# One-core hybrid decoder step: the feed-forward's opening as one piece in a fixed order, and five plain pairs of up tiles instead of four

## The chip, the core and the metric

One core of one Trainium2 chip runs the whole program. The metric is the device time of one execution in microseconds (us). TensorE does the matrix products, VectorE and ScalarE the elementwise work, GpSimd small copies and some adds, and SyncE issues the DMA transfers. In the profile they are PE (PEld for its weight loads), DVE, ACT, POOL and SP.

## What is computed

The reference is one inference step of a 2-layer decoder trunk on 576 tokens (512 of a prompt, 64 of eight running sequences), width 1024. Each layer has a token-mixing part and a feed-forward part. The change touches the feed-forward alone, all in float32:

```python
xn = rms_norm(x, p['g_pre_ffn'])
u = xn @ p['w_up']                        # 1024 -> 5632
ext = concatenate([conv_prev, u], axis=1)
c = sum(ext[:, j:j + L] * p['w_conv'][j] for j in range(3))
a, b = split(c, 2, axis=-1)
ffn = (gelu(a, approximate=True) * b) @ p['w_down']   # 2816 -> 1024
x = x + rms_norm(ffn, p['g_post_ffn'])
```

## The kernel before

Every float32 matrix is split into a high and a low part in a faster matmul type, and a product is three matmuls: high by high, low by high, high by low. ScalarE makes the high part of a weight tile (a copy, L113), VectorE the low part (a subtraction, L114, `split_w`).

The 5632 up columns are 44 tiles of 128, worked in 22 pairs; a pair's even tile is `a` and its odd tile `b`. The first `NPLAIN` = 4 pairs (tiles 0 to 7) are *plain*: eight weight blocks by three matmuls, over the tokens in two halves of 320 and 256 columns, each half in one of three PSUM banks (`main_bank`, three buffers). VectorE brings a half out of PSUM (L1055, an *evacuation*: two instructions for the first half, one for the second), multiplying by the norm factor `R`. The other 18 pairs are *fast* (`fast_pair`): a Strassen-like scheme makes the pair with seven products of half size in 288 columns (L1162 to L1164; 12 matmuls each) in place of eight. It needs combinations of the weights (`weights`: four additions, four splits) and combinations of the activations, made once a layer by `combine(0..3)`: two normalizations (L1117), four quarter operations (L1118 to L1121), four high parts on ScalarE (L1125) and four low parts on VectorE (L1126), from the x tiles, with the y tiles as scratch.

After a tile is complete, `conv_end` copies its last columns into `cso` on GpSimd (L1068, L1069), ScalarE makes the first tap (L1075), and VectorE adds the other two (L1076, L1077, the *convolution sums*). After the odd tile of a pair `h_tile` follows: gelu on ScalarE (L1086), multiplication on VectorE (L1087), and a split (L1097, L1098). The tile's input buffer `u` has four buffers and is begun by `conv_begin` with a GpSimd copy and a memset (L1041, L1042); the output buffer `c` has two. So tile n's evacuation waits until tile n-4 has had its convolution.

Tiles 0 to 2 are done together in `first_tiles`, inside the end of the token-mixing part. Then `up(j)` runs for each pair, with the down product's tiles (`down`) set between by `FF_AFTER`: in the first group of down tiles, two after each of pairs 4 to 7. `copy_cache` issues two 768 KB cache copies after each pair.

A planner orders the instructions of each engine by a simulated timeline, within data dependences and hand-written edges (`behind`). Inside `tc.manual_schedule(engines=ORDERED)` the instructions of VectorE, ScalarE and GpSimd keep the order in which they are written; TensorE and the DMA queue stay with the planner. Before the change only `boundary_half` uses it. `combine(i)` stands after tile i+3 and behind the newest weight low part.

Of the kernel before, what the change touches and what calls it, by code (L numbers as in the profile page):

```python
# [19 lines left out]
P = 128  # L20
# [59 lines left out]
def trunk_kernel(ctx: ExitStack, tc: tile.TileContext, I, O):  # L80
# [929 lines left out]
    def ffn(l, y, xpool, act, first):  # L1010
# [20 lines left out]
        with ExitStack() as fx:  # L1031
# [6 lines left out]
            def conv_begin(ui):  # L1038
# [14 lines left out]
                def plain(b, hf, t0, n):  # L1053
                    r = R[:, t0:t0 + n]
                    place(t0, n, lambda d, c: V.tensor_tensor(d, c(b), c(r), ALU.mult))  # L1055
                    if hf:
                        conv_end(ui)

                def fast(hf, op, last=False):
                    place(hf * SH, SH, op)  # L1060
# [2 lines left out]
                return plain, fast  # L1063

            def conv_end(ui):
                u = us.pop(ui)
                uv = u[:, 0:80].rearrange("p (b t) -> p b t", t=10)
                G.tensor_copy(cso[:, ui, 0:16].rearrange("p (b t) -> p b t", t=2), uv[:, :, 8:10])  # L1068
                G.tensor_copy(cso[:, ui, 16:18], u[:, NU - 2:NU])  # L1069
                c = cp.tile([P, NU - 2], F32, name="c", tag="c", bufs=2)  # L1070

                def wc(i):
                    o = PR_WC + (l * 2 * NJ + ui) * 3 + i
                    return par[:, o:o + 1]
                S.activation(c, u[:, 0:NU - 2], AF.Copy, scale=wc(0))  # L1075
                V.scalar_tensor_tensor(c, u[:, 1:NU - 1], wc(1), c, ALU.mult, ALU.add)  # L1076
                V.scalar_tensor_tensor(c, u[:, 2:NU], wc(2), c, ALU.mult, ALU.add)  # L1077
                cs[ui] = c
                if ui % 2:
                    h_tile(ui // 2)  # L1080

            hh, hl = [None] * NJ, [None] * NJ

            def h_tile(j):
                ca, cb = cs.pop(2 * j), cs.pop(2 * j + 1)
                S.activation(ca, ca, AF.Gelu_apprx_tanh)  # L1086
                V.tensor_tensor(cb, ca, cb, ALU.mult)  # L1087
# [3 lines left out]
                for hf, d0, d1, c0, c1 in ((0, 0, TS, 0, 80), (0, TS, 320, 80, 336), (1, 0, 256, 336, NU - 2)):  # L1091
                    src, dh, dl = cb[:, c0:c1], hh[j][hf][:, d0:d1], hl[j][hf][:, d0:d1]
                    if c0 == 0:
                        src = src.rearrange("p (b t) -> p b t", t=10)[:, :, 0:8]
                        dh = dh.rearrange("p (b t) -> p b t", t=8)
                        dl = dl.rearrange("p (b t) -> p b t", t=8)
                    S.activation(dh, src, AF.Copy)  # L1097
                    V.tensor_tensor(dl, src, dh.bitcast(F32), ALU.subtract)  # L1098

# [9 lines left out]
            HW = WN // 2  # L1109
            xs, sw = [], None  # L1110

            def combine(i):

                with behind(last_lo[0].ins):
                    x1, x2, ua, ta = (y[4 * (i % 2) + m] for m in range(4))
                    for k, d in ((i, x1), (i + HK, x2)):
                        V.scalar_tensor_tensor(d, xt[k], gnorm(l, 2, k), R, ALU.mult, ALU.mult)  # L1117
                    V.tensor_tensor(ua[:, :SH], x1[:, :SH], x1[:, SH:], ALU.subtract)  # L1118
                    V.scalar_tensor_tensor(ua[:, SH:], x2[:, SH:], -1.0, ua[:, :SH], ALU.mult, ALU.subtract)
                    V.tensor_tensor(ta[:, :SH], x2[:, SH:], x1[:, SH:], ALU.subtract)  # L1120
                    V.scalar_tensor_tensor(ta[:, SH:], ua[:, SH:], -1.0, x2[:, :SH], ALU.mult, ALU.subtract)  # L1121
                    hi, lo = (cp.tile([P, 7 * SH], F32R, name=f"{n}{i}", tag=f"{n}{i}") for n in ("sxh", "sxl"))
                    for src, m, n in ((x1[:, :SH], B11, 1), (x2, B21, 2), (ua, U1, 2), (ta, T3, 2)):
                        cols = slice(m * SH, (m + n) * SH)
                        S.activation(hi[:, cols], src, AF.Copy)  # L1125
                        V.tensor_tensor(lo[:, cols], src, hi[:, cols].bitcast(F32), ALU.subtract)  # L1126
                    xs.append((hi, lo))

            def weights(j):

                r0, r1 = (wp.tile([P, WN], F32, name="wraw", tag="wraw", bufs=3) for _ in range(2))
                for i, r in enumerate((r0, r1)):
                    with behind(last_w[0].ins):
                        last_w[0] = SP.dma_start(r, I["w_up"][l, 2 * j + i])
                ws = cp.tile([P, WN], F32, name="ws", tag="ws")
                a, b = slice(0, HW), slice(HW, WN)
                w0 = split_w(r0, WN, sw, 2)
                V.tensor_tensor(ws[:, b], r0[:, a], r1[:, a], ALU.add)
                V.tensor_tensor(r1[:, a], r1[:, a], r1[:, b], ALU.add)
                V.tensor_tensor(ws[:, a], r0[:, a], r1[:, a], ALU.add)  # L1140
                w2 = split_w(ws, WN)
                w1 = split_w(r1, WN, sw, 2)
                V.tensor_tensor(r0[:, b], r0[:, b], ws[:, a], ALU.add)
                w3 = split_w(r0[:, b], HW)
                return w0, w1, w2, w3

            def fast_pair(j):
                with behind(last_lo[0].ins if j == NPLAIN else None):
                    w0, w1, w2, w3 = weights(j)
                e1, e2 = (conv_begin(2 * j + i)[1] for i in range(2))  # L1150
                with behind(last_mm[0].ins if j == NPLAIN else None):
                    products(w0, w1, w2, w3, e1, e2)

            def products(w0, w1, w2, w3, e1, e2):

# [27 lines left out]
                product(ba, w1, 1, T4, True)  # L1183
                e2(0, lambda d, c: S.activation(d, c(ba), AF.Copy, scale=-1.0), True)

            def up(j):
                if j >= NPLAIN:
                    fast_pair(j)
                else:
                    for ui in (2 * j, 2 * j + 1):  # L1190
                        if ui >= NFIRST:
                            col_tile(load_w(I["w_up"][l, ui]), xh, xl, allk, conv_begin(ui)[0])
                            if ui in COMBINE:
                                combine(COMBINE.index(ui))
                copy_cache()
                copy_cache()

# [9 lines left out]
                col_tile(w, hh, hl, list(range(j0, j0 + nj)), evac)  # L1207

            first_tiles(first, act, [conv_begin(i)[0] for i in range(NFIRST)])
            for j in range(NJ + 1):  # L1210
                if j < NJ:
                    up(j)
                    if j == NPLAIN - 1:

                        xpool.release()
                        sw = right_pool(f"sw{l}")
                else:
                    cp.release()
                    sw.release()
# [228 lines left out]
```

## Time and profile before

| what | value |
|---|---|
| time, median of 3 runs (lowest to highest) | 1683.43 us (1682.94 to 1683.83) |
| the profiled execution: its time, its span | 1681.14 us, 1679.4 us |
| mean granted TensorE clock | 0.985 |
| busy: PE, DVE, ACT, POOL | 1606.9, 1248.1, 877.6, 556.9 us |

How to read it: the span runs from the first to the last instruction; the granted clock is the share of full speed that the chip gave to TensorE (1.00 is 2.4 GHz, 0.50 is 1.2 GHz). Matmuls overlap, so the length listed for one is longer than the step to the next; the steps between starts are what a stretch costs. The same holds for VectorE and ScalarE, whose listed lengths overlap by a little under 0.1 us. Layer 0's feed-forward opens at 446 us and layer 1's at 1277 us.

### The profile page before, as it was taken

To read this page: it belongs to the slowest core of one execution; us is meant where nothing else is said; L and a number is where in the kernel's file an instruction comes from. 1 tells how busy PE (TensorE), PEld (TensorE's weight loads), DVE (VectorE), ACT (ScalarE), POOL (GpSimd) and SP (SyncE) were. 2 spreads that over 40 slices of the span, in tenths; PEclk is the share of its full clock that TensorE was granted. 3 is DMA by queue.
4 is the path that set the end of the run, shared out by engine and by line. 5 is a ranking of instruction groups with operands and counts; after the bars stand their busy time and mean duration, and the time that the engine had idled before them with its cause. 6 is when DMAs were issued, how large, how long until landed. Compare 5 with 4: busy or idle time off the path is not lost.

```text
span 1679.4 us, 35933 instructions
## 1 busy us (share of the span) xinstructions
PE 1606.9 (96%) x14256; PEld 1526.1 (91%) x14256; DVE 1248.1 (74%) x2472; ACT 877.6 (52%) x1638; POOL 556.9 (33%) x800
## 2 busy tenths in 40 slices
PE   8999999999979999999989999989999799999997
PEld 7888997789879999999988899968998799999997
DVE  6775765656898888888757757566568978888985
ACT  6754524564556545555456544255735555555541
POOL 4554332302542111221365553332044411212303
PEclk9999999999989999999999999999999899999999
DMA  5221326848424545653522212378474264456432
GB/s 187 71 71 59 103 100 258 298 181 313 142 102 164 212 159 171 220 200 105 174 80 84 78 65 80 120 280 336 159 272 157 82 213 157 171 200 242 149 119 104
DMA packets 74889, 270.36 MB, mean 161 GB/s; under 512 B 10689, under 2 KB 23265, under 8 KB 73185
## 3 DMA queue, kind: packets, MB, share of 16 engines
q1 hardware_dynamic: 74720, 268.07, 45.0%
q8 instruction: 112, 1.84, 0.4%
q14 instruction: 57, 0.46, 0.1%
HBM read 250.11 MB, written 85.02 MB: 200 GB/s over the span
## 4 chain that ended last, share of the span: by engine, by line
PE 76%; DVE 10%; ACT 5%; POOL 3%; issue 3%; DMA 2%; POOLq 0%; SPq 0%; ACTq 0%; DVEq 0%
PE ps_m L132 14%; PE ps_m L134 13%; PE ps_m L133 13%; PE ps_m L1164 4%; PE ps_m L1162 4%; PE ps_m L1163 4%; DVE wlo L114 2%; PE ps_t L1163 2%; PE ps_t L1164 2%; PE ps_t L1162 2%; PE ps_s L493 2%; DMA wraw<-in_w_up 1%; PE ps_o L965 1%; PE ps_o L869 1%; POOL x L352 1%
## 5 line engine op out<-in xcount | busy, mean ns | idle before, releaser
L113 ACT ACTIVATE whi<-wraw 128x1024 fp32r<-128x1024 f32 (+4 forms) x284 | 247.0, 877 | 209.2 <-PE ps_m L133 55.4
L114 DVE TENSOR_TENSOR wlo<-wraw,whi 128x1024 fp32r<-128x1024 f32 (+4 forms) x284 | 285.4, 1010 | 94.6 <-ACT whi L113 88.3
L132 PE MATMUL ps_m<-xha,whi 128*128 128x320 f32 x864 | 272.4, 316 | 5.4 <-ACT whi L113 3.1
L133 PE MATMUL ps_m<-xla,whi 128*128 128x320 f32 x864 | 270.9, 314 | 0.0
L134 PE MATMUL ps_m<-xha,wlo 128*128 128x320 f32 x864 | 268.4, 314 | 0.5 <-DVE wlo L114 0.5
L132 PE MATMUL ps_m<-xm,whi 128*128 128x256 f32 x864 | 248.6, 288 | 18.5 <-DVE u L1055 18.5
L134 PE MATMUL ps_m<-xm,wlo 128*128 128x256 f32 x864 | 247.8, 287 | 0.0
L133 PE MATMUL ps_m<-xm,whi 128*128 128x256 f32 x864 | 246.9, 286 | 0.0
L132 PEld LDWEIGHTS ps_m<-xm,whi 128*128 128x128 f32 x864 | 165.9, 192 | 22.0 <-issue 20.5
L132 PEld LDWEIGHTS ps_m<-xha,whi 128*128 128x128 f32 x864 | 164.1, 190 | 9.5 <-ACT whi L113 4.3
L1162 PE MATMUL ps_m<-sxh,whi 128*128 128x288 f32 x576 | 170.0, 296 | 0.7 <-ACT acc L1168 0.7
L1163 PE MATMUL ps_m<-sxh,wlo 128*128 128x288 f32 x576 | 169.7, 295 | 0.0
L1164 PE MATMUL ps_m<-sxl,whi 128*128 128x288 f32 x576 | 169.7, 295 | 0.0
L133 PEld LDWEIGHTS ps_m<-xm,whi 128*128 128x128 f32 x864 | 166.1, 192 | 1.5 <-issue 1.1
L134 PEld LDWEIGHTS ps_m<-xm,wlo 128*128 128x128 f32 x864 | 166.1, 192 | 1.1 <-issue 0.2
L133 PEld LDWEIGHTS ps_m<-xla,whi 128*128 128x128 f32 x864 | 164.3, 190 | 2.5 <-issue 2.0
L134 PEld LDWEIGHTS ps_m<-xha,wlo 128*128 128x128 f32 x864 | 163.3, 190 | 2.8 <-issue 1.4
L1069 POOL COPY cso<-u 128x2 f32<-128x2 f32 x88 | 74.4, 845 | 268.3 <-DVE u L1180 199.5
L1162 PEld LDWEIGHTS ps_m<-sxh,whi 128*128 128x128 f32 x576 | 108.4, 188 | 1.2 <-ACT acc L1168 1.2
L1163 PEld LDWEIGHTS ps_m<-sxh,wlo 128*128 128x128 f32 x576 | 108.7, 189 | 0.0
L1164 PEld LDWEIGHTS ps_m<-sxl,whi 128*128 128x128 f32 x576 | 108.3, 188 | 0.0
L1041 POOL COPY u<-cso 128x16 f32<-128x16 f32 x88 | 59.8, 682 | 136.7 <-DVE c L1077 86.9
(342 smaller groups left out, 4187.6 us busy)
## 6 DMA issues: line engine op xcount, KB each, us to landing
wraw<-in_w_up SPq DMA_DIRECT2D x88, 512.0 KB, 3.8
kv<-in_ck SPq DMA_DIRECT2D x32, 768.0 KB, 6.6
kv<-in_cv SPq DMA_DIRECT2D x32, 768.0 KB, 7.0
out_ck<-in_ck SPq DMA_DIRECT2D x32, 768.0 KB, 7.7
out_cv<-in_cv SPq DMA_DIRECT2D x32, 768.0 KB, 6.8
wraw<-in_w_s SPq DMA_DIRECT2D x42, 512.0 KB, 3.6
wraw<-in_w_dn SPq DMA_DIRECT2D x48, 256.0 KB, 2.6
x<-xdr SPq DMA_DIRECT2D x24, 288.0 KB, 6.4
```

What stands on the lines that cost most here:

```text
L113: S.activation(hi[:, :n], raw[:, :n], AF.Copy)
L114: last_lo[0] = V.tensor_tensor(lo[:, :n], raw[:, :n], hi[:, :n].bitcast(F32), ALU.subtract)
L132: PE.matmul(out, ah, bh, start=(i == 0), stop=False)
L133: PE.matmul(out, ah, bl, start=False, stop=False)
L134: last_mm[0] = PE.matmul(out, al, bh, start=False, stop=(i == n - 1))
L352: (V if dram_out and k % 4 == 3 else G).tensor_tensor(xk, xk, yk, ALU.add)
L493: mm = PE.matmul(bp[64 * hh:64 * hh + 64, cp * nh * 32:(cp + 1) * nh * 32], xk[:, c0:c0 + 64], moving(c0), start=True, stop=True)
L1041: G.tensor_copy(uv[:, :, 0:2], cso[:, ui, 0:16].rearrange("p (b t) -> p b t", t=2))
L1069: G.tensor_copy(cso[:, ui, 16:18], u[:, NU - 2:NU])
L1162: PE.matmul(b, wh, xh, start=i == 0 and not more, stop=False, skip_group_check=more)
L1163: PE.matmul(b, wl, xh, start=False, stop=False, skip_group_check=more)
L1164: PE.matmul(b, wh, xl, start=False, stop=i == HK - 1, skip_group_check=more)
```

## The change

`FF_AFTER`, `NPLAIN` and `COMBINE` change, and the opening (from the end of `first_tiles` to the weights of the first fast pair) is written out as one function under `manual_schedule`. `conv_end` is cut into `taps` and `conv_sums`, `h_tile` into `h_gelu`, `h_mult` and `h_split` (all three high parts first, then all three low parts), `combine` into `normalize`, `combine` and `lows`, and `weights` yields once half way. Pair 4 becomes plain, so the fast pairs are 5 to 21. The ten cache copies of the first five pairs are issued behind the opening, and the first down tiles follow pair 5 (two), 6 (three) and 7 (three).

```diff
-FF_AFTER = ({4: 2, 5: 2, 6: 2, 7: 2}, {8: 2, 9: 2, 10: 2, 11: 2}, {12: 2, 13: 2, 14: 2, 15: 2},
+FF_AFTER = ({5: 2, 6: 3, 7: 3}, {8: 2, 9: 2, 10: 2, 11: 2}, {12: 2, 13: 2, 14: 2, 15: 2},
             {17: 1, 18: 1, 19: 1, 20: 1, 22: 4})
-NPLAIN = 4
-COMBINE = (3, 4, 5, 6)
+NPLAIN = 5
...
+            def taps(*uis):
+                for ui in uis:
+                    u = us[ui]
+                    uv = u[:, 0:80].rearrange("p (b t) -> p b t", t=10)
+                    G.tensor_copy(cso[:, ui, 0:16].rearrange("p (b t) -> p b t", t=2), uv[:, :, 8:10])
+                    G.tensor_copy(cso[:, ui, 16:18], u[:, NU - 2:NU])
+                    cs[ui] = cp.tile([P, NU - 2], F32, name="c", tag="c", bufs=2)
+                    S.activation(cs[ui], u[:, 0:NU - 2], AF.Copy, scale=tap_weight(ui, 0))
+
+            def conv_sums(*uis):
+                for i in (1, 2):
+                    for ui in uis:
+                        c = cs[ui]
+                        V.scalar_tensor_tensor(c, us[ui][:, i:NU - 2 + i], tap_weight(ui, i), c, ALU.mult, ALU.add)
+                for ui in uis:
+                    del us[ui]
...
+            def normalize(i):
+                x1, x2, ua, ta = (y[4 * (i % 2) + m] for m in range(4))
+                for k, d in ((i, x1), (i + HK, x2)):
+                    V.scalar_tensor_tensor(d, xt[k], gnorm(l, 2, k), R, ALU.mult, ALU.mult)
...
+            def combine(i, parts, tiles):
+                x1, x2, ua, ta = tiles
+                V.tensor_tensor(ua[:, :SH], x1[:, :SH], x1[:, SH:], ALU.subtract)
+                V.tensor_tensor(ta[:, :SH], x2[:, SH:], x1[:, SH:], ALU.subtract)
+                V.scalar_tensor_tensor(ua[:, SH:], x2[:, SH:], -1.0, ua[:, :SH], ALU.mult, ALU.subtract)
+                V.scalar_tensor_tensor(ta[:, SH:], ua[:, SH:], -1.0, x2[:, :SH], ALU.mult, ALU.subtract)
+                for src, m, n in parts:
+                    S.activation(xs[i][0][:, m * SH:(m + n) * SH], src, AF.Copy)
+
+            def lows(i, parts):
+                for src, m, n in parts:
+                    cols = slice(m * SH, (m + n) * SH)
+                    V.tensor_tensor(xs[i][1][:, cols], src, xs[i][0][:, cols].bitcast(F32), ALU.subtract)
...
                 w2 = split_w(ws, WN)
+                yield
                 w1 = split_w(r1, WN, sw, 2)
                 V.tensor_tensor(r0[:, b], r0[:, b], ws[:, a], ALU.add)
                 w3 = split_w(r0[:, b], HW)
-                return w0, w1, w2, w3
+                yield w0, w1, w2, w3
...
+            def opening():
+                ws, bs, evs = {}, {}, {}
+                halves = [(ui, hf) for ui in range(NFIRST, 2 * NPLAIN) for hf in range(2)]
+                def load(*uis):
+                    for ui in uis:
+                        ws[ui] = load_w(I["w_up"][l, ui])
+                def mm():
+                    ui, hf = halves.pop(0)
+                    col_half(ws[ui], xh, xl, allk, hf, lambda *a: bs.__setitem__((ui, hf), a))
+                def ev(*keys):
+                    for key in keys:
+                        if key[1] == 0:
+                            evs[key[0]] = conv_begin(key[0])[0]
+                        evs[key[0]](*bs.pop(key))
+                        if halves:
+                            mm()
+                with tc.manual_schedule(engines=ORDERED):
+                    load(3, 4, 5)
+                    c = [normalize(0)]
+                    taps(0, 1)
+                    for _ in range(3):
+                        mm()
+                    conv_sums(0, 1)
+                    h_gelu(0)
+                    ev((3, 0))
+                    combine(0, *c[0])
+                    lows(0, c[0][0])
+                    h_mult(0)
+                    ev((3, 1))
+                    h_split(0)
+                    ev((4, 0))
+                    load(6)
+                    c.append(normalize(1))
+                    combine(1, *c[1])
+                    taps(2, 3)
+                    ev((4, 1))
+                    conv_sums(2, 3)
+                    h_gelu(1)
+                    ev((5, 0))
+                    lows(1, c[1][0])
+                    load(7)
+                    ev((5, 1), (6, 0))
+                    h_mult(1)
+                    c.append(normalize(2))
+                    combine(2, *c[2])
+                    h_split(1)
+                    load(8)
+                    ev((6, 1))
+                    lows(2, c[2][0])
+                    taps(4, 5)
+                    ev((7, 0))
+                    load(9)
+                    ev((7, 1))
+                    conv_sums(4, 5)
+                    h_gelu(2)
+                    c.append(normalize(3))
+                    combine(3, *c[3])
+                    xpool.release()
+                    sw = right_pool(f"sw{l}")
+                    ev((8, 0))
+                    lows(3, c[3][0])
+                    h_mult(2)
+                    ev((8, 1), (9, 0))
+                    w = weights(NPLAIN)
+                    next(w)
+                    ev((9, 1))
+                    h_split(2)
+                    early[NPLAIN] = next(w)
+                for ui in range(6, 2 * NPLAIN):
+                    conv_end(ui)
+                for _ in range(2 * NPLAIN):
+                    copy_cache()
...
             first_tiles(first, act, [conv_begin(i)[0] for i in range(NFIRST)])
-            for j in range(NJ + 1):
+            opening()
+            for j in range(NPLAIN, NJ + 1):
```

## Rows read from the trace of the kernel before

**Rows 1.** Stretch; busy us (x instructions) of PE, PEld, DVE, ACT, POOL; granted clock; DMA share, GB/s.

```profile
475.00:480.00 5.00, 0.37 (x3) 0.11 (x1) 5.00 (x9) 2.40 (x4) 1.46 (x1) 0.85 0.00 0
...
485.00:490.00 5.00, 5.00 (x28) 5.00 (x29) 5.00 (x12) 3.04 (x7) 3.17 (x2) 0.62 0.01 3
...
1280.00:1320.00 40.00, 31.39 (x220) 31.15 (x220) 40.00 (x76) 20.35 (x34) 17.20 (x18) 0.88 0.33 126
```

**Rows 2.** Timeline of PE: start, length, what, [idle before it <- releaser]; both holes.

```profile
484.95 0.55 PE L132 MATMUL ps_m<-xm,whi 128*128 128x256 f32 x1 [9.58 <-DVE u L1055]
...
1316.08 0.55 PE L132 MATMUL ps_m<-xm,whi 128*128 128x256 f32 x1 [8.61 <-DVE u L1055]
...
1321.13 0.41 PE L134 MATMUL ps_m<-xm,wlo 128*128 128x256 f32 x1
```

**Rows 3.** Timeline of PE, the two shorter gaps of layer 0's opening.

```profile
462.34 0.35 PE L132 MATMUL ps_m<-xm,whi 128*128 128x256 f32 x1 [0.34 <-DVE u L1055]
...
505.43 0.41 PE L132 MATMUL ps_m<-xha,whi 128*128 128x320 f32 x1 [0.56 <-ACT u L1184]
```

**Rows 4.** Timeline of PE: first matmuls of tile 3, of tile 7, of two products.

```profile
445.98 0.39 PE L132 MATMUL ps_m<-xha,whi 128*128 128x320 f32 x1
...
471.69 0.31 PE L132 MATMUL ps_m<-xha,whi 128*128 128x320 f32 x1
...
489.58 0.29 PE L1162 MATMUL ps_m<-sxh,whi 128*128 128x288 f32 x1
...
491.17 0.29 PE L1162 MATMUL ps_s<-sxh,whi 128*128 128x288 f32 x1
```

**Rows 5.** Timeline of DVE where layer 0's opening begins.

```profile
443.67 3.50 DVE L114 TENSOR_TENSOR wlo<-wraw,whi 128x1024 fp32r<-128x1024 f32 x3
...
447.08 0.75 DVE L1055 TENSOR_TENSOR u<-ps_s,rbc 128x256 f32<-128x256 f32 x2
```

**Rows 6.** Timeline of DVE, one of each kind of step (xN: N together).

```profile
448.07 3.00 DVE L1117 SCALAR_TENSOR_TENSOR y<-x,par,rbc 128x576 f32<-128x576 f32 x4
...
478.70 1.21 DVE L114 TENSOR_TENSOR wlo<-wraw,whi 128x1024 fp32r<-128x1024 f32 x1
...
479.84 0.45 DVE L1119 SCALAR_TENSOR_TENSOR y<-y,y 128x288 f32<-128x288 f32 x1
...
481.71 0.75 DVE L1126 TENSOR_TENSOR sxl<-y,sxh 128x576 fp32r<-128x576 f32 x1
...
482.38 0.82 DVE L1077 SCALAR_TENSOR_TENSOR c<-u,par,c 128x592 f32<-128x592 f32 x1
...
484.26 0.88 DVE L1055 TENSOR_TENSOR u<-ps_m,rbc 128x64 f32<-128x64 f32 x3
...
487.36 0.77 DVE L1087 TENSOR_TENSOR c<-c 128x592 f32<-128x592 f32 x1
...
489.78 0.55 DVE L1098 TENSOR_TENSOR xla<-c,xha 128x64 fp32r<-128x64 f32 x2
...
506.35 1.23 DVE L114 TENSOR_TENSOR wlo<-wraw,whi 128x1024 fp32r<-128x1024 f32 x1 [0.16 <-ACT whi L113]
```

**Rows 7.** Timeline of ACT: tap, high parts of activations, high part of weights.

```profile
447.53 1.47 ACT L1075 ACTIVATE c<-u,par 128x592 f32<-128x592 f32 x2 [0.89 <-DVE u L1055]
...
449.65 1.18 ACT L1125 ACTIVATE sxh<-y 128x576 fp32r<-128x576 f32 x2 [0.28 <-DVE y L1117]
...
505.26 1.06 ACT L113 ACTIVATE whi<-wraw 128x1024 fp32r<-128x1024 f32 x1
```

**Rows 8.** Timeline of POOL: the copy that begins tile 6's buffer.

```profile
478.54 3.97 POOL L1041 COPY u<-cso 128x16 f32<-128x16 f32 x1 [6.77 <-DVE c L1077]
```

**Rows 9.** The same view, a stretch in which the DMA engines are full.

```profile
515.00:520.00 5.00, 5.00 (x41) 5.00 (x40) 3.07 (x4) 2.89 (x6) 0.00 (x0) 1.00 1.12 411
```

**Rows 10.** The same view, at the start of layer 1's opening.

```profile
1275.00:1280.00 5.00, 3.68 (x18) 3.48 (x17) 5.00 (x8) 2.78 (x5) 2.60 (x4) 0.72 0.50 151
```

**Rows 11.** Timeline of PE, the gap in that stretch.

```profile
1276.64 0.71 PE L276 MATMUL ps_t<-con,rr 128*128 128x128 f32 x4 [1.32 <-POOL rr L250]
```

More of the change, by code (lines that the diff above doesn't have):

```diff
@@ L1065, in conv_end @@
             def conv_end(ui):
[L1066 to L1074, printed above, removed]
@@ new lines, in conv_end, with tap_weight @@
+                conv_sums(ui)
+                if ui % 2:
+                    j = ui // 2
+                    h_gelu(j)
+                    h_mult(j)
+                    h_split(j)
+            def tap_weight(ui, i):
+                o = PR_WC + (l * 2 * NJ + ui) * 3 + i
+                return par[:, o:o + 1]
+            def taps(*uis):
[6 more added lines that the diff above has]
+                    S.activation(cs[ui], u[:, 0:NU - 2], AF.Copy, scale=tap_weight(ui, 0))
@@ new lines, in conv_sums, with h_gelu, h_mult @@
+            def conv_sums(*uis):
[5 more added lines that the diff above has]
+                    del us[ui]
+            hh, hl = [None] * NJ, [None] * NJ
+            def h_gelu(j):
+                S.activation(cs[2 * j], cs[2 * j], AF.Gelu_apprx_tanh)
+            def h_mult(j):
+                V.tensor_tensor(cs[2 * j + 1], cs[2 * j], cs[2 * j + 1], ALU.mult)
@@ L1089, in h_tile, with h_split @@
+            def h_split(j):
+                cb = cs.pop(2 * j + 1)
+                del cs[2 * j]
                 i = j % NH
                 _, hh[j], hl[j] = two_parts(fp, i) if i < NEX else two_parts(xp, i - NEX)
[L1091 to L1098, printed above, removed]
+                for part in range(2):
+                    for hf, d0, d1, c0, c1 in ((0, 0, TS, 0, 80), (0, TS, 320, 80, 336), (1, 0, 256, 336, NU - 2)):
+                        src, dh, dl = cb[:, c0:c1], hh[j][hf][:, d0:d1], hl[j][hf][:, d0:d1]
+                        if c0 == 0:
+                            src = src.rearrange("p (b t) -> p b t", t=10)[:, :, 0:8]
+                            dh = dh.rearrange("p (b t) -> p b t", t=8)
+                            dl = dl.rearrange("p (b t) -> p b t", t=8)
+                        if part == 0:
+                            S.activation(dh, src, AF.Copy)
+                        else:
+                            V.tensor_tensor(dl, src, dh.bitcast(F32), ALU.subtract)
@@ L1110, in ffn @@
             xs, sw = [], None
[L1112 to L1127, printed above, removed]
@@ new lines, in normalize @@
+            def normalize(i):
+                x1, x2, ua, ta = (y[4 * (i % 2) + m] for m in range(4))
+                for k, d in ((i, x1), (i + HK, x2)):
+                    V.scalar_tensor_tensor(d, xt[k], gnorm(l, 2, k), R, ALU.mult, ALU.mult)
+                xs.append([cp.tile([P, 7 * SH], F32R, name=f"{n}{i}", tag=f"{n}{i}") for n in ("sxh", "sxl")])
+                return ((x1[:, :SH], B11, 1), (x2, B21, 2), (ua, U1, 2), (ta, T3, 2)), (x1, x2, ua, ta)
+            def combine(i, parts, tiles):
[6 more added lines that the diff above has]
+                    S.activation(xs[i][0][:, m * SH:(m + n) * SH], src, AF.Copy)
@@ L1144, in weights @@
                 w3 = split_w(r0[:, b], HW)
-                return w0, w1, w2, w3
+                yield w0, w1, w2, w3
             def fast_pair(j):
-                with behind(last_lo[0].ins if j == NPLAIN else None):
-                    w0, w1, w2, w3 = weights(j)
-                e1, e2 = (conv_begin(2 * j + i)[1] for i in range(2))
+                w = early.pop(j, None)
+                if w is None:
+                    *_, w = weights(j)
                 with behind(last_mm[0].ins if j == NPLAIN else None):
-                    products(w0, w1, w2, w3, e1, e2)
+                    products(*w, *(conv_begin(2 * j + i)[1] for i in range(2)))
             def products(w0, w1, w2, w3, e1, e2):
@@ L1184, in products @@
                 e2(0, lambda d, c: S.activation(d, c(ba), AF.Copy, scale=-1.0), True)
-            def up(j):
[L1187 to L1194, printed above, removed]
+            early = {}
@@ L1195, in up @@
+            def up(j):
+                fast_pair(j)
                 copy_cache()
```

16 lines of the change are left out of this document (2 added, 14 removed).

## The prediction, made before the changed kernel was run

> **What bounds the kernel now.** I read the busy shares of the page first: TensorE is busy 96% of the span, so only its gaps and its clock can be won, and the slices of the span show its weak places. Two of them lie in the feed-forward's openings, one per layer. Then the windows: in both openings VectorE is busy without a break while TensorE stands still [rows 1]. The timeline of TensorE gives the hole: it stops in tile 7 for 9.58 us in layer 0 and 8.61 us in layer 1, each time released by the evacuation (L1055) of an earlier half, and when it starts again the granted clock is low: a mean of 0.62 over 485 to 490 us, part of it at 1.2 GHz (0.50) and part at 2.4 (1.00) [rows 1, 2]. Two shorter gaps stand beside it in layer 0, of 0.34 and 0.56 us; layer 1 has one like the second [rows 3].
>
> The clock costs as well. In 485 to 490 us, 0.38 x 5 = 1.9 us were lost. In layer 1 the 24 matmuls from 1316.08 to 1321.13 take 5.05 / 23 x 24 = 5.3 us; at full clock 12 matmuls of 288 columns take 1.59 us [rows 4], so 24 of 256 columns take 2.8, and 2.4 were lost. Together the openings lose 9.58 + 0.34 + 0.56 + 1.9 = 12.4 us in layer 0 and 8.61 + 0.56 + 2.4 = 11.6 in layer 1: **24.0 us** is all that can be won here.
>
> Why is the evacuation late? VectorE has work ahead of it that nobody waits for yet (combinations, weight sums), and tile 6's buffer began late: its GpSimd copy took 3.97 us [rows 8]. But VectorE is never idle there. An order cannot shrink its work; it can only put first what TensorE needs.
>
> **The change, part by part.** *Plain for fast.* A plain tile takes (471.69 - 445.98 - 0.34) / 4 = 6.34 us of TensorE [rows 3, 4], a pair 12.7; seven products of 1.59 take 11.1. The change adds 1.6 us of TensorE work per layer. *The plain tiles as cover.* TensorE now has seven plain tiles behind tile 2, not five: work from 445.98 to 490.4 before it must have a combination.
>
> *VectorE's work up to the first product.* It must be done in the written order up to the first weight low part of pair 5. Steps are taken from start to start, which is the listed length less about 0.08 us [rows 6]: normalization 0.73, quarter operation 0.37, low part 0.67 for 576 columns and 0.37 for 288 (as a quarter), convolution sum 0.74, weight low part 1.14, multiplication 0.69, evacuation of a tile 0.80 (0.46 and 0.34), low parts of a split 0.47 + 0.34. From 447.08, where it takes up the first tiles' second halves [rows 5], the list is:
> three second halves 1.0; four combinations of 2 x 0.73 + 4 x 0.37 + 0.37 + 3 x 0.67 = 5.3, so 21.3; twelve convolution sums 8.9; three multiplications 2.1; two splits 1.6; low parts of tiles 6 to 9, 4.6; evacuations of seven tiles but for the last half 5.3; the low part itself 1.1. The sum is **45.9 us**.
>
> *Waits that the order itself makes.* ScalarE keeps its order too: a high part of 576 columns is 0.59, a tap 0.69, a weight's high part 0.96, and a hand-over between the engines adds some 0.1 [rows 6, 7]. Where VectorE's next step needs a result that stands behind others in ScalarE's queue, it waits, and all behind it waits. I walked the list for such places. Before the sums of tile 2: two high parts, the tap and hand-overs (2.1) against one quarter operation and one half evacuation (0.7), 1.4. Before the split of pair 1: two high parts and the first piece against one quarter operation, 1.2. Before tile 8's low part 0.6, and twice 0.15 inside splits. That is 3.5, so the low part ends at 447.08 + 45.9 + 3.5 = 496.5, and TensorE, which started 0.3 us after the release it waited for (evacuations from 484.26, matmul at 484.95) [rows 2, 6], begins the products at 496.8. Its gaps until then are 496.8 - 490.4 = **6.4 us**, in pieces of at most 2.2, since evacuations now come between the combinations.
>
> *The rest of the opening.* After it VectorE has three sums (0.60 each, an estimate from the 576-column row), the second weight's low part, the last evacuation, the split of pair 2, two more low parts and a sum: 6.4, with waits of 1.2 and 0.7 for high parts. Then tiles 6 and 7 must be convolved (3.0) before pair 5's buffers are free, and two evacuations (0.8) before the seventh product: 496.5 + 12.1 + 0.3 = 508.9. TensorE can run six products (9.5) by 506.3, so **2.8 us** more gap (0.2 left out). From there two, three and three down tiles cover the backlog of tiles 8 and 9.
>
> *GpSimd's copies* cost nothing if each begins while VectorE does something that lets it pass; the dearest is 3.97 [rows 8]. In the new order an evacuation follows soon after each convolution, and a waiting VectorE frees it. *The ten cache copies* (7.9 MB) are 19 us at 411 GB/s [rows 9]; behind the last weight load, at some 481, they end at 500, and the down tiles' weights are needed at about 509. I take nothing; without that cover the down tiles come up to 10 us late. *The weight loads* of tiles 6 to 9 and of pair 5 go, as before, into the buffer that the low part three tiles earlier frees, by the walk 10 us and more before they are used: nothing. *The low parts of tiles 3 to 5* lie, as now, in VectorE's gap from 443.67 [rows 5]: nothing.
>
> **Sum.** Per layer 6.4 + 2.8 + 1.6 = 10.8, twice 21.6, against 24.0: **-2.4 us**. On the profiled execution's 1681.14 us that is 1678.7; the median of the runs lies 2.3 higher, at 1683.43, so 1681.0.
>
> Where it can lie: with no waits on ScalarE at all the products begin at 493.3 (gap 2.9), and the seventh product waits 0.7, so 5.6 less per layer. With hand-overs of 0.3 in place of 0.1, some ten on the path, 2 more.
>
> **The rivals.** *A. The walk holds* (0.40): 1681.0, own range 1677 to 1686. *B. ScalarE is never late* (0.25): the walk's waits are filled or shorter. In full 2 x 5.6 more, so 1670; by half 1675. For it speaks that VectorE worked through layer 1's 40 us without a wait [rows 1]; against it, that this was an order made to avoid waits.
>
> *C. The block starts late* (0.13): if tiles 3 to 5 are split only after the first tiles' evacuations, VectorE loses 443.67 to 447.08, 3.4 us, at a point from which it is the bound, and tile 3 starts 3.4 later. Twice 3.4: +6.8 - 2.4 = 4.4 slower, 1687.8. It decides if the first weight low part of the block begins after 447.1. Against it: the halves of the evacuation need `R`, which comes later than the weights.
>
> *D. The clock falls in the small gaps* (0.12). Layer 1's opening fell to 0.72 with no gap above 1.32 us [rows 10, 11]; the walk has 3 us of gaps in the 6 from 494.9. At 1.9 to 2.4 a layer the result is +1.4 to +2.4: 1685 to 1686. The Trainium skill (TensorE: Matmul & The Clock Gate, A second HAM failure mode: psum-queue depth-cycling) describes a kernel whose frequent short idles between groups of matmuls made the clock swing; by that rule both layers pay; if only holes like those of [rows 2] bring the clock down, neither does.
>
> *E. A GpSimd copy holds a tile* (0.10). A copy of 3.97 in place of 0.2 on the path, once a layer, is +7.5 - 2.4: 1688.5. The row shows it outlasting several VectorE instructions [rows 6, 8]. The Trainium skill (SBUF — State Buffer, Who interferes with whom) has a VectorE instruction with two SBUF inputs block a GpSimd read for its whole length; by one instruction it would be 1.1 at most and the sum would move by 2. Against E: VectorE itself waits for that copy, and then gives way.
>
> **The numbers.** A gives faster, same and slower 0.13, 0.24, 0.03; B is faster; C 0.01 same and 0.12 slower; D 0.08 and 0.04; E 0.03 and 0.07. Together 0.38, 0.36, 0.26, where 0.2% (3.4 us) is about what a measurement of this kernel tells from no change. The range 1671 to 1689 leaves out the end of B and mixtures of C with D.
>
> **What would show it.** In the trace after: no gap of TensorE above 2.5 us in either opening; the first product near 497 us and the first of layer 1 some 830 later (the two holes end 831 apart [rows 2]); VectorE waiting for ScalarE about five us in each; the clock at 1.00 from 455 to 515. It is wrong if VectorE waits elsewhere than I listed, if the first half of tile 8 waits over 3 us, or if the down tiles wait for their weights.

## The result, and the profile after

| | before | after |
|---|---|---|
| median of 4 runs each (lowest to highest) | 1683.18 us (1681.22 to 1683.83) | 1695.26 us (1692.94 to 1697.10) |
| ratio, 95% interval | | 1.0065 (1.0048 to 1.0083) |
| span of the profiled execution | 1679.4 us | 1695.3 us |

The change costs 12 us, outside the range that was given. Both layers pay alike. From the first matmul of the opening (`con,rr`) to the first evacuation of the last fast pair, the timelines give 332.7 and 333.4 us before and 340.5 and 341.1 after. That is 7.7 us a layer, 15.5 of the 15.9 between the two spans.

TensorE's timeline of the changed kernel, all gaps in layer 0's opening and the largest one of layer 1's:

```profile
480.96 0.38 PE L131 MATMUL ps_m<-xha,whi 128*128 128x320 f32 x1 [1.68 <-DVE u L1054]
...
491.77 0.36 PE L131 MATMUL ps_m<-xm,whi 128*128 128x256 f32 x1 [0.66 <-DVE u L1054]
...
496.66 0.40 PE L1188 MATMUL ps_m<-sxh,wlo 128*128 128x288 f32 x1 [1.20 <-DVE wlo L113]
...
501.05 0.40 PE L1187 MATMUL ps_m<-sxh,whi 128*128 128x288 f32 x1 [1.21 <-ACT whi L112]
...
502.31 0.40 PE L1188 MATMUL ps_m<-sxh,wlo 128*128 128x288 f32 x1 [0.86 <-DVE wlo L113]
...
505.01 0.40 PE L1188 MATMUL ps_t<-sxh,wlo 128*128 128x288 f32 x1 [0.84 <-DVE wlo L113]
...
515.37 0.63 PE L131 MATMUL ps_m<-xha,whi 128*128 128x320 f32 x1 [3.85 <-ACT whi L112]
...
1354.62 0.64 PE L131 MATMUL ps_m<-xha,whi 128*128 128x320 f32 x1 [3.47 <-ACT whi L112]
```

The first six are the fixed order. The holes of 9.58 and 8.61 us [rows 2] are gone. In their place stand pieces of at most 1.68, and the first product waits for its weight's low part until 496.66. The prediction had said 496.8. VectorE's timeline shows the waits for ScalarE that the prediction had listed as 1.4, 1.2, 0.6 and 1.2, and one more at the end:

```profile
465.12 3.08 DVE L1088 SCALAR_TENSOR_TENSOR c<-u,par,c 128x592 f32<-128x592 f32 x4 [1.18 <-ACT c L1082]
...
477.69 0.73 DVE L1116 TENSOR_TENSOR xla<-c,xha 128x64 fp32r<-128x64 f32 x2 [0.98 <-ACT xha L1114]
...
479.25 1.23 DVE L113 TENSOR_TENSOR wlo<-wraw,whi 128x1024 fp32r<-128x1024 f32 x1 [0.49 <-ACT whi L112]
...
501.03 1.23 DVE L113 TENSOR_TENSOR wlo<-ws,whi 128x1024 fp32r<-128x1024 f32 x1 [1.12 <-ACT whi L112]
...
515.35 0.69 DVE L113 TENSOR_TENSOR wlo<-wraw,whi 128x512 fp32r<-128x512 f32 x1 [3.84 <-ACT whi L112]
```

That last one, and TensorE's gap of 3.85 us beside it, belong to the first down tile. Both name ScalarE's high part (L112) as the releaser, but ScalarE was itself waiting. Its timeline names the transfer:

```profile
514.69 0.63 ACT L112 ACTIVATE whi<-wraw 128x512 fp32r<-128x512 f32 x1 [4.60 <-DMA wraw<-in_w_dn]
```

The timeline of the DMA queue (SP; start, length from the first issue to the end of the last with the waits between, xN: N transfers) says why that load is late:

```profile
472.20 8.63 SPq L1158 DMA_DIRECT2D wraw<-in_w_up  x2
480.88 13.88 SPq L1028 DMA_DIRECT2D out_ck<-in_ck  x12
496.35 8.97 SPq L119 DMA_DIRECT2D wraw<-in_w_dn  x2
```

Twelve cache copies are issued in one go: the opening's ten and the two that follow pair 5, 9.4 MB. Of the 13.88 us, SyncE waits 6.3 for earlier copies to land. Its waits from 480.5 to 495 us (total, times, longest), then the last copy with its time to landing:

```profile
SPq L1028 <- DMA out_ck<-in_ck: 6.3, 4, 2.2
...
494.25 0.51 SPq L1028 DMA_DIRECT2D out_ck<-in_ck  x1
DMA to landing us min/median/max: 19.5/19.5/19.5
```

Taken one by one, the first eight copies go out one after the other, some 0.6 us each (one took 1.04). The ninth goes out at 486.87, when the first has landed (6.0 us after 480.88), and the tenth to twelfth follow the second to fourth. The first down load goes out at 496.35, in good time, but seven copies (5.5 MB) are still on their way, and the last of them lands at 494.25 + 19.5 = 513.8. ScalarE gets the load at 514.69, 18.3 us after its issue. The page, the chain that ended last by line and then two rows of the issues (their last number is the median time to landing):

```profile
PE ps_m L131 13%; PE ps_m L133 13%; PE ps_m L132 13%; PE ps_m L1187 3%; PE ps_m L1188 3%; PE ps_m L1189 3%; DVE wlo L113 2%; DMA wraw<-in_w_dn 2%; PE ps_s L492 2%; PE ps_t L1188 2%; PE ps_t L1189 2%; PE ps_t L1187 2%; DMA wraw<-in_w_up 2%; PE ps_o L964 1%; DVE c L1088 1%
...
out_ck<-in_ck SPq DMA_DIRECT2D x32, 768.0 KB, 11.7
...
wraw<-in_w_dn SPq DMA_DIRECT2D x48, 256.0 KB, 2.6
```

The loads of down weights now stand on the chain with 2% of the span: two loads of some 18 us are 36 us, and that is 2% of 1695. The median of such a load is still 2.6 us, so the row of the issues doesn't show them. The windows of the changed kernel (columns as in [rows 1]) show what the DMA engines moved meanwhile, and a second price:

```profile
445.00:450.00 5.00, 4.78 (x23) 4.78 (x24) 5.00 (x9) 3.12 (x4) 0.85 (x6) 0.66 0.73 237
...
480.00:520.00 40.00, 30.35 (x198) 28.81 (x199) 34.49 (x62) 17.97 (x32) 7.00 (x21) 0.93 0.93 309
...
500.00:505.00 5.00, 2.26 (x13) 1.81 (x13) 3.97 (x9) 3.79 (x8) 0.44 (x2) 1.00 1.08 298
...
510.00:515.00 5.00, 1.52 (x12) 1.29 (x10) 1.51 (x3) 0.40 (x2) 0.31 (x1) 0.91 0.82 277
515.00:520.00 5.00, 4.63 (x18) 4.63 (x19) 4.65 (x7) 3.84 (x8) 1.47 (x3) 0.50 0.81 303
520.00:525.00 5.00, 5.00 (x37) 5.00 (x36) 3.04 (x8) 2.12 (x6) 0.63 (x2) 0.90 0.58 213
```

Over 40 us the DMA engines were nearly full (share 0.93) and moved 309 GB/s in all, not 411. After the wait TensorE starts at a granted clock of 0.50, which is 1.2 GHz. The loss is 0.50 x 4.63 + 0.10 x 5.00 = 2.8 us. So one layer pays 3.85 + 2.8 = 6.7 us; layer 1, with a gap of 3.47 and windows of 0.50 and 0.94 behind it, pays 3.47 + 2.5 + 0.3 = 6.3. Together that is 13.0 of the 15.5 us between the two profiled executions; the other 2.5 are not accounted for.

### The profile page after: what moved, and what is told of

It is laid out like the page before. It is cut to its first block, busy times and chain, and to the rows that moved or that the text cites. A ratio compares the mean times of both kernels' runs of the same rounds, so it can differ in the third digit from the quotient of the medians.

```text
span 1695.3 us, 35939 instructions
## 1 busy us (share of the span) xinstructions
PE 1618.5 (95%) x14280; PEld 1534.0 (90%) x14280; DVE 1243.2 (73%) x2464; ACT 871.3 (51%) x1624; POOL 533.2 (31%) x800
## 4 chain that ended last, share of the span: by engine, by line
PE 74%; DVE 11%; ACT 6%; DMA 5%; POOL 3%; issue 2%; SPq 0%; POOLq 0%; DVEq 0%; ACTq 0%
PE ps_m L131 13%; PE ps_m L133 13%; PE ps_m L132 13%; PE ps_m L1187 3%; PE ps_m L1188 3%; PE ps_m L1189 3%; DVE wlo L113 2%; DMA wraw<-in_w_dn 2%; PE ps_s L492 2%; PE ps_t L1188 2%; PE ps_t L1189 2%; PE ps_t L1187 2%; DMA wraw<-in_w_up 2%; PE ps_o L964 1%; DVE c L1088 1%
## 5 line engine op out<-in xcount | busy, mean ns | idle before, releaser
L112 ACT ACTIVATE whi<-wraw 128x1024 fp32r<-128x1024 f32 (+4 forms) x282 | 245.2, 878 | 190.3 <-PE ps_m L132 52.5
L131 PE MATMUL ps_m<-xha,whi 128*128 128x320 f32 x896 | 285.1, 319 | 15.3 <-ACT whi L112 10.4
L132 PE MATMUL ps_m<-xla,whi 128*128 128x320 f32 x896 | 283.1, 316 | 0.0
L133 PE MATMUL ps_m<-xha,wlo 128*128 128x320 f32 x896 | 280.5, 316 | 0.6 <-DVE wlo L113 0.5
L131 PE MATMUL ps_m<-xm,whi 128*128 128x256 f32 x896 | 256.9, 287 | 1.3 <-DVE u L1054 1.3
L132 PE MATMUL ps_m<-xm,whi 128*128 128x256 f32 x896 | 255.4, 285 | 0.0
L131 PEld LDWEIGHTS ps_m<-xm,whi 128*128 128x128 f32 x896 | 171.4, 191 | 4.2 <-issue 1.8
L132 PEld LDWEIGHTS ps_m<-xm,whi 128*128 128x128 f32 x896 | 171.7, 192 | 1.6 <-issue 1.1
L1188 PE MATMUL ps_m<-sxh,wlo 128*128 128x288 f32 x544 | 161.0, 296 | 4.1 <-DVE wlo L113 4.1
L1187 PE MATMUL ps_m<-sxh,whi 128*128 128x288 f32 x544 | 161.3, 297 | 3.7 <-ACT whi L112 2.4
L1189 PE MATMUL ps_m<-sxl,whi 128*128 128x288 f32 x544 | 160.5, 296 | 0.0
L1088 DVE SCALAR_TENSOR_TENSOR c<-u,par,c 128x592 f32<-128x592 f32 x176 | 144.3, 829 | 5.4 <-ACT c L1082 4.6
L1080 POOL COPY cso<-u 128x2 f32<-128x2 f32 x88 | 48.7, 553 | 259.5 <-DVE u L1205 169.9
```

What stands on the lines that cost most here:

```text
L112: S.activation(hi[:, :n], raw[:, :n], AF.Copy)
L131: PE.matmul(out, ah, bh, start=(i == 0), stop=False)
L132: PE.matmul(out, ah, bl, start=False, stop=False)
L133: last_mm[0] = PE.matmul(out, al, bh, start=False, stop=(i == n - 1))
L1088: V.scalar_tensor_tensor(c, us[ui][:, i:NU - 2 + i], tap_weight(ui, i), c, ALU.mult, ALU.add)
L1187: PE.matmul(b, wh, xh, start=i == 0 and not more, stop=False, skip_group_check=more)
```

## The experiments

The first question was whether the twelve copies are the whole loss, or whether the fixed order or the fifth plain pair also costs. Each ratio is against the kernel before, measured beside it on the same chip, where its median was 1684.5 to 1685.6 us; so the ratios say more than the times. Edits are against the changed kernel unless another is named.

**The copies between the loads.** Two stand behind `load(3, 4, 5)` and two behind each of `load(6)` to `load(9)`; none stand behind the opening.

```diff
                     load(3, 4, 5)
+                    copy_cache()
+                    copy_cache()
...
                     load(6)
+                    copy_cache()
+                    copy_cache()
...
                 for ui in range(6, 2 * NPLAIN):
                     conv_end(ui)
-                for _ in range(2 * NPLAIN):
-                    copy_cache()
```

> The changed kernel, but its ten cache copies go two by two between the weight loads of the opening and not in one burst behind it. Theory 1 (the burst holds back the down tiles' weights and pair 6's weights; each layer's opening ends some 8 us later for it, slow clock included): 1677 to 1683 us, no wait of ScalarE for a down tile's weights above 1 us in the openings, and TensorE's gaps near the 9 us per layer of the walk. Theory 2 (VectorE's fixed order and the extra plain pair cost the time, the late weights only fill time that would be lost anyway): 1692 to 1697 us. In between, 1685 to 1690, if both.

Measured: 1683.35 us, just above the range of theory 1, ratio 0.9998 (0.9987 to 1.0009). The queue now issues two copies after each load, and the same gaps of the fixed order are there. Queue, then TensorE:

```profile
482.14 1.15 SPq L1028 DMA_DIRECT2D out_ck<-in_ck  x2
486.07 20.52 SPq L119 DMA_DIRECT2D wraw<-in_w_dn  x2
```

```profile
482.21 0.38 PE L131 MATMUL ps_m<-xha,whi 128*128 128x320 f32 x1 [1.68 <-DVE u L1054]
...
497.92 0.40 PE L1188 MATMUL ps_m<-sxh,wlo 128*128 128x288 f32 x1 [1.20 <-DVE wlo L113]
```

The waits for down weights are gone, and with them the whole loss: 1.0065 against 0.9998 is 11.3 us. In layer 0 the first evacuation of pair 8 comes 118.6 us after the opening's first matmul, against 126.3 in the changed kernel: 7.7 us, where 6.7 were worked out above. What is left of the change measures as nothing.

**The copies later.** The opening issues none; a third copy follows each pair from 8 on. It was run twice.

```diff
                 copy_cache()
                 copy_cache()
+                if j > 7:
+                    copy_cache()
```

> The changed kernel without copies in the opening: the ten follow later, one more behind each of the pairs from 8 on. Theory 1: 1676 to 1682 us, like the run with copies between the loads or a little under it, as no copy then shares the DMA engines with the opening's weight loads. Theory 2: 1692 to 1697 us. If copies between the loads cost as well, this one is faster than that one by more than 3 us.

> The run with the copies later once more, beside the next one on the same chip: 1680 to 1684 us, a ratio to before of 0.998 to 1.000.

Measured: 1682.95 us, ratio 0.9988 (0.9974 to 1.0003), and 1683.82, 0.9995 (0.9984 to 1.0006); the first time lies above its range. With no copy in the way at all it is no better than with two behind each load: what counts is that they do not stand together.

**The burst in the kernel before.** The same twelve copies at one point, behind the weights of pair 5; the order and the plain pairs stay as they were.

```diff
-                copy_cache()
-                copy_cache()
+                for _ in range(0 if j < 5 else 12 if j == 5 else 2):
+                    copy_cache()
```

> The kernel before with only its cache copies moved: those of pairs 0 to 5, twelve in all, go in one burst behind pair 5's weights. Everything else stays. Theory 1: the weights of the down tiles behind pair 5 come late here too, 5 to 8 us per layer, 1692 to 1699 us. Theory 2, in which a burst is hidden: 1682 to 1685 us.

Measured: 1703.18 us, ratio 1.0112 (1.0091 to 1.0132), more than either theory expected. The queue's timeline, and TensorE's:

```profile
493.31 13.18 SPq L1029 DMA_DIRECT2D out_ck<-in_ck  x12
508.53 2.20 SPq L120 DMA_DIRECT2D wraw<-in_w_dn  x2
```

```profile
526.51 0.64 PE L132 MATMUL ps_m<-xha,whi 128*128 128x320 f32 x1 [3.64 <-ACT whi L113]
```

The burst makes the same wait in a kernel without the rest of the change. From pair 5 to pair 6 (first evacuations) this kernel takes 23.6 and 24.2 us, against 17.35 in both layers before: 13.1 of the 19 us. Layer 1's gap there is 4.96 us. From pair 6 to pair 8 another 3.8 are lost, in the two layers together; the remaining 2 are open.

**Seven in the burst.** Five copies between the loads and five behind the opening, where pair 5's two join them.

```diff
-                for _ in range(2 * NPLAIN):
+                for _ in range(5):
                     copy_cache()
```

> The changed kernel with five of the ten cache copies between the loads and five in the burst, so seven with pair 5's own, not twelve. Theory 1 in its form with a cover (twelve copies ran from 481 to 515 us, some 2.8 us each; seven end near 501, before the down tiles' weights are wanted near 509): 1681 to 1686 us, as with none in the burst. If each copy in a burst costs by itself, whatever the cover: 7/12 of the 12 us, 1689 to 1692.

Measured: 1683.56 us, ratio 0.9994 (0.9980 to 1.0007), and no wait for down weights. The queue:

```profile
479.78 4.86 SPq L1028 DMA_DIRECT2D out_ck<-in_ck  x7
484.74 19.48 SPq L119 DMA_DIRECT2D wraw<-in_w_dn  x2
```

So a burst does not cost by its length. Of the seven copies (5.5 MB) the last lands 14.8 us after its issue, at 498.9, before the down weights are used, and they cost nothing; of the twelve the last lands at 513.8, and they cost all of it.

**The ten behind the down loads.** In the changed kernel the ten copies move behind the two down loads that follow pair 5.

```diff
-                for _ in range(2 * NPLAIN):
-                    copy_cache()
...
+                if j == NPLAIN:
+                    for _ in range(2 * NPLAIN):
+                        copy_cache()
```

> The changed kernel with its ten copies moved by two loads: behind the two weight loads of the down tiles after pair 5 instead of ahead of them (pair 5's own two copies stay). Theory 1 (whatever stands behind the burst in the one DMA queue comes late): the down tiles' weights now come in time, and pair 6's weights, wanted some 9 us later, are behind ten copies that start near 505 us and run 28 us: TensorE waits 8 to 16 us per layer before pair 6, 1696 to 1715 us. Rival (only the down tiles' weights matter, since ScalarE's high part of them blocks its queue): 1682 to 1687 us.

Measured: 1726.35 us, ratio 1.0250 (1.0235 to 1.0265), far more than expected. TensorE's timeline, the queue's, and the waits between 500 and 560 us (total, times, longest):

```profile
536.47 0.61 PE L1187 MATMUL ps_m<-sxh,whi 128*128 128x288 f32 x1 [17.33 <-ACT whi L112]
```

```profile
506.62 9.38 SPq L1028 DMA_DIRECT2D out_ck<-in_ck  x10
517.42 2.24 SPq L1158 DMA_DIRECT2D wraw<-in_w_up  x2
```

```profile
ACT whi L112 <- DMA wraw<-in_w_up: 17.1, 2, 11.6
```

The down tiles get their weights, and now pair 6's up weights stand behind the burst. They are issued at 517.42, and TensorE wants them 17.33 us before 536.47, at 519.1; the down load of the changed kernel was issued 14 us before ScalarE was free for it. So the gap is 17.33 us and not 3.85, and 15.81 in layer 1. Whatever is behind the burst pays, and by how soon it is needed.

**The planner's order.** The kernel with the copies between the loads, with the planner choosing the order on VectorE, ScalarE and GpSimd:

```diff
-                with tc.manual_schedule(engines=ORDERED):
+                with nullcontext():
```

> The changed kernel with copies between the loads, and the opening written the same way, but its order on VectorE, ScalarE and GpSimd left to the planner. Theory 1, with the walk of the prediction: the planner puts work that nobody waits for ahead of evacuations again, a hole of 4 to 9 us per layer in place of the small gaps, and a fall of the clock behind it: 1681 to 1690 us, at least 2 us above the run with copies between the loads. Theory 2, in which the fixed order itself costs: below that run by 3 us or more.

Measured: 1685.98 us, ratio 1.0009 (0.9995 to 1.0023). The holes come back, in both layers:

```profile
484.69 0.55 PE L131 MATMUL ps_m<-xm,whi 128*128 128x256 f32 x1 [7.62 <-DVE u L1054]
...
1319.58 0.55 PE L131 MATMUL ps_m<-xm,whi 128*128 128x256 f32 x1 [9.27 <-DVE u L1054]
```

Against the 0.9998 of the same kernel in the fixed order, that order would be worth about 0.1%, but most of the two intervals is common to both, so the times do not show it. The traces show that the holes of [rows 2] come from the planner's order, and that closing them wins much less than their length: VectorE's work is the same, and the fixed order leaves 6.4 us of smaller gaps a layer.

**Five plain pairs alone.** The kernel before, with `NPLAIN` = 5 and the new `FF_AFTER`:

```diff
-NPLAIN = 4
+NPLAIN = 5
```

> The kernel before with only its counts changed: five plain pairs, and the first down tiles after pairs 5 (two), 6 and 7 (three each). Order and copies stay the planner's and the old ones. If the extra plain pair only costs its TensorE work (1.6 us per layer): 1686 to 1688 us. If it also gives VectorE the room that it lacks, and the hole shrinks by as much or more: 1680 to 1685. If theory 2 is right and the pair is what costs in the changed kernel: above 1690.

Measured: 1683.93 us, ratio 0.9997 (0.9985 to 1.0009). The holes on TensorE are there, a little shorter than those of [rows 2]:

```profile
483.44 0.55 PE L132 MATMUL ps_m<-xm,whi 128*128 128x256 f32 x1 [7.63 <-DVE u L1055]
...
1315.65 0.55 PE L132 MATMUL ps_m<-xm,whi 128*128 128x256 f32 x1 [8.29 <-DVE u L1055]
```

They are 18.2 - 15.9 = 2.3 us shorter in sum, and the two gaps of 0.56 us before the first down tiles [rows 3] are gone: 3.4 us, against 3.2 us of added matrix work. The fifth plain pair is no part of the loss.

**An order without the waits.** With the copies later, steps are set so that VectorE has other work while ScalarE makes what it needs next: taps before the combination, the split of pair 1 and an evacuation before the third one, and two evacuations ahead of the low parts. It was run twice.

```diff
                     c.append(normalize(1))
-                    combine(1, *c[1])
                     taps(2, 3)
+                    combine(1, *c[1])
...
-                    combine(2, *c[2])
                     h_split(1)
                     load(8)
                     ev((6, 1))
-                    lows(2, c[2][0])
+                    combine(2, *c[2])
                     taps(4, 5)
                     ev((7, 0))
+                    lows(2, c[2][0])
...
                     c.append(normalize(3))
+                    ev((8, 0))
                     combine(3, *c[3])
...
-                    ev((8, 0))
                     lows(3, c[3][0])
```

> The run with the copies later, with its order changed where VectorE waits for ScalarE's queue or an evacuation comes late: the taps of tiles 2 and 3 ahead of combination 1's high parts, the split of pair 1 and tile 8's load and tile 6's last evacuation ahead of combination 2, tile 8's first evacuation ahead of combination 3. The walk with the new order has 2.8 us less of TensorE's gaps per layer: 1676 to 1679 us, and only the gap before the first product (some 3 us) and those between the products stay. Rival: VectorE's work alone sets the first product's time and the gaps only move: 1681 to 1685.

> The order without the waits once more. The walk: 2.8 us per layer under the run with the copies later, 1676 to 1680 us, a ratio to before of 0.995 to 0.998. Rival: the first run's 0.9975 was chance, and the ratio is that of the run beside it within 0.1%.

Measured: 1679.26 us, ratio 0.9975 (0.9958 to 0.9991), and 1681.85, 0.9982 (0.9966 to 0.9998): a little faster than both kernels, though both times lie above their ranges. Against the two runs with the copies later it wins 0.13% each time, 2.2 us; the intervals overlap. In layer 0 the low part of the third product's weights is there 55.4 and 55.2 us after the opening's first matmul, against 57.1 with the copies later and in the changed kernel: 1.7 to 1.9 us, where the walk had 2.8. In the first of the two, three gaps are left, 3.3 us in sum where there were 6.4. TensorE's timeline and the windows of the first of the two:

```profile
493.29 0.40 PE L1187 MATMUL ps_m<-sxh,whi 128*128 128x288 f32 x1 [0.51 <-DVE u L1054]
494.89 0.60 PE L1188 MATMUL ps_m<-sxh,wlo 128*128 128x288 f32 x1 [1.20 <-DVE wlo L113]
...
501.52 0.43 PE L1188 MATMUL ps_m<-sxh,wlo 128*128 128x288 f32 x1 [1.56 <-DVE wlo L113]
```

```profile
495.00:500.00 5.00, 4.96 (x23) 4.55 (x23) 3.32 (x7) 2.44 (x6) 0.56 (x2) 0.67 0.01 3
500.00:505.00 5.00, 3.48 (x15) 3.48 (x16) 5.00 (x10) 2.62 (x5) 0.65 (x2) 0.68 0.07 13
```

The clock falls to 0.67 and 0.68 with no gap above 1.56 us near it, some 0.33 x 5 + 0.32 x 3.5 = 2.8 us of TensorE's time. What this costs is not shown: in the second run, with 0.66 and 1.00 in these two windows, pair 6's first evacuation comes 77.6 us after the opening's first matmul, and in this one 77.1.

**One weight sum earlier.** The same, with the fourth sum of every fast pair's weights ahead of a split:

```diff
                 V.tensor_tensor(ws[:, a], r0[:, a], r1[:, a], ALU.add)
+                V.tensor_tensor(r0[:, b], r0[:, b], ws[:, a], ALU.add)
                 w2 = split_w(ws, WN)
```

> The run before this one with the fourth weight sum moved ahead of the second split, in every pair: VectorE does it while ScalarE makes the high part, so the third product's wait falls by 0.6 us or less in each layer, and nothing else changes where TensorE is the bound: 0 to 2 us under the run without the waits, 1675 to 1679 us. Rival: what VectorE saves before the third product it pays before the fourth, so no difference within 1 us.

Measured: 1682.71 us, above its range, ratio 0.9989 (0.9977 to 1.0002). In layer 0 the third product's low part is there after 54.7 us, 0.6 sooner than in the order without it, as expected, but no gain is seen in the time; the intervals overlap, so a loss isn't shown either.

## Why the prediction was wrong

**What bounds it, and what could be won**: right. The holes come from VectorE's order, and they close when it is fixed.

**The walk**: right up to the first product. Its weight part came at 496.66 for 496.8; the waits for ScalarE measured 1.18, 0.98, 0.49 and 1.12 for 1.4, 1.2, 0.6 and 1.2, and the last one, 0.7, did not occur. The 6.4 us of gaps until then measured 1.68 + 0.66 + 1.20 = 3.54. Of the difference, 0.34 x 4.78 = 1.6 us is a fall of the clock to 0.66 in the first five microseconds: TensorE was busy for longer with the same work, so it waited less for VectorE. The 2.8 us behind the first product (508.9 less 506.3 is 2.6) measured 1.21 + 0.86 + 0.84 = 2.91, but in another place, so that the size agrees is luck. The walk had them before the seventh product, which would wait for the convolutions of tiles 6 and 7; in the trace the third and fourth wait for weights, since two convolution sums (L1088) come between pair 5's weight sums:

```profile
497.13 0.83 DVE L1088 SCALAR_TENSOR_TENSOR c<-u,par,c 128x592 f32<-128x592 f32 x1
...
498.48 0.83 DVE L1088 SCALAR_TENSOR_TENSOR c<-u,par,c 128x592 f32<-128x592 f32 x1
```

The walk's -2.4 us is to be held against the kernels without the burst: ratios of 0.9998, 0.9988 and 0.9995 are -0.3, -2.0 and -0.8 us. All three intervals reach beyond -2 us and beyond zero. The sign of that small sum is not settled; that it is small is.

**The fifth plain pair**, +1.6 us a layer: not seen in the time. It shortened the gaps by about as much, 3.4 us for 3.2.

**The ten cache copies**: this step failed. It ran: "*The ten cache copies* (7.9 MB) are 19 us at 411 GB/s [rows 9]; behind the last weight load, at some 481, they end at 500, and the down tiles' weights are needed at about 509. I take nothing; without that cover the down tiles come up to 10 us late." The start (480.88) and the need (509; ScalarE was free for the high part at 510.09) were right. Two numbers between them were wrong:
- The count. Pair 5's own two copies stand directly behind the ten, ahead of the down loads: twelve, 9.4 MB.
- The rate. 411 GB/s was read from 5 us with a DMA share of 1.12 [rows 9], the crest of a slice. Over 40 us of nearly full engines it is 309.

Twelve copies at 309 GB/s are 30.5 us and end at 511.4; in the trace the last lands at 513.8 and the load behind it is there 0.9 us later. By the same sum either error alone would just have been covered: ten at 309 end at 506.4, twelve at 411 at 503.8. No run tried either, and in the trace the tenth copy lands at 509.1, so for ten the cover is used up. The prediction had named the price in its last sentence, and the wait as what would show it wrong, but gave the case no chance of its own, so none of the five rivals holds it. The late load cost 3.85 and 3.47 us directly and, which the price did not have, 2.8 us a layer of lower clock behind it: 13.0 us by the trace, 11.3 by the ratios. The runs with the copies between, later, or seven in a burst show it by taking the loss away, and the burst in the kernel before by making it.

The Trainium skill (DMA: Bandwidth & Descriptors, Queues, rings and completion order) says that SyncE's transfers share one row of rings and that each DMA engine consumes its descriptors in ring order. The trace agrees: a load of 256 KB issued with seven copies ahead of it was there 18.3 us later, 0.9 us behind the last of them.

**The rivals.** A held but for the copies. B (ScalarE never late) was a matter of the order: the better order wins 2.2 us over the runs with the copies later, if the two pairs of runs are taken at their word, where that rival in full would have given 11.2 more than A. C did not occur: VectorE begins the low parts of tiles 3 to 5 at 443.38, ahead of 447.1. D did not occur where it was placed: from 495 to 510 us the changed kernel's clock held 1.00. It fell at the gap of 1.32 us ahead of the opening, in both layers after (0.66) and in one before (0.72), and among the short gaps of the better order (0.66 to 0.68). E did not occur: no gap of the opening is released by a GpSimd copy.

## What to carry to other kernels

When bulk transfers are moved in a shared queue, list what is issued behind them up to the first load that something waits for, with every transfer that the code around adds at the same place. Cost the whole group at a rate averaged over a long full stretch, and give "the load behind it is late" its own chance and price. Copies that nobody waits for are best set two by two behind loads that are early; and a wait on TensorE is priced with the stretch of lower clock after it, where TensorE is what sets the pace.

## What the runs showed of the hardware

- The copies' price did not go by their number: seven in a burst cost nothing, twelve 11.3 us, and ten ahead of a load that is needed at once 41 us. What counted is when the load behind them was needed.
- In the burst of twelve the copies landed one after the other, the first 6.0 us after its issue and the last 19.5; from 486.9 to 513.8 that is one every 2.4 us. In the three kernels with ten or twelve in one go SyncE waited for a landing before the ninth and each later one; with seven it did not. Without such a wait the issue of a copy takes some 0.6 us. Whether the program or the chip sets that limit of eight is not shown.
- The same gap of 1.32 us at the opening's start was followed by a full clock in some executions and not in others. The kernel with the copies later, profiled twice, held 1.00 in both layers in one profile and fell to 0.70 (445 to 450 us) and 0.72 (1274 to 1280) in the other. With TensorE busy for 3.98 and 4.68 us there, that is 1.2 and 1.3 us of its time, and still it cost nothing: from the opening's first matmul to the fourth product of layer 0 it is 504.25 - 444.46 = 59.79 us in the one and 505.80 - 446.02 = 59.78 in the other. VectorE sets the pace there, and at full clock TensorE waits for it in two more gaps, 0.70 and 0.75 us. The windows (columns as in [rows 1]) and TensorE's timeline, full clock first:

```profile
445.00:450.00 5.00, 5.00 (x39) 5.00 (x38) 5.00 (x9) 3.14 (x4) 0.67 (x5) 1.00 0.87 297
445.00:450.00 5.00, 3.98 (x19) 3.98 (x20) 5.00 (x8) 2.87 (x5) 1.64 (x6) 0.70 0.60 190
```

```profile
444.46 0.71 PE L275 MATMUL ps_t<-con,rr 128*128 128x128 f32 x4 [1.32 <-POOL rr L249]
...
504.25 0.40 PE L1188 MATMUL ps_t<-sxh,wlo 128*128 128x288 f32 x1 [0.83 <-DVE wlo L113]
```

```profile
446.02 0.71 PE L275 MATMUL ps_t<-con,rr 128*128 128x128 f32 x4 [1.32 <-POOL rr L249]
...
505.80 0.40 PE L1188 MATMUL ps_t<-sxh,wlo 128*128 128x288 f32 x1 [0.83 <-DVE wlo L113]
```
